# A Hymba-style encoder block: paired rests turned in the bank of the fourth turned tile, an earlier low-rank load, reordered steps, and more bridging products

## The chip, the cores and the metric

One Trainium2 chip; the kernel runs on one of its cores. The metric is the device time of one execution in microseconds. The kernel before takes 905.07 us, the median of 3 runs (904.97 to 905.77).

## What is computed

One layer over 512 tokens of width 2048, in float32. A condition vector gives shift, scale and gate; the normalised and modulated input is projected once, and the columns go to two mixers, dilated sliding-window attention (16 heads of 64) and gated linear attention (4 heads, GLA below). Both are gated, joined and projected out.

```python
mod = jax.nn.silu(c) @ w_cond[layer] + b_cond[layer]
shift, scale, gate = jnp.split(mod, 3, axis=-1)
h = rms_norm(x) * (1.0 + scale[:, None]) + shift[:, None]
proj = h @ w_in[layer]
aq, ak, av, ag, gq, gk, gv, gg, lr_f, lr_b = jnp.split(proj, PROJ_SPLITS, axis=-1)
...
for window, dilation in DILATED_PATTERNS:        # (128,1), (512,4), (2048,16)
    o_p, lse_p = dilated_window_attention(aq, ak, av, rel_bias, window, dilation)
...
g_o = rms_norm(o_fwd + o_bwd).reshape(B, S, GLA_WIDTH) * gla_norm_gain[layer]
g_out = g_o * jax.nn.silu(gg)
y = jnp.concatenate([a_out, g_out], axis=-1) @ w_out[layer]
x = x + gate[:, None] * y
return rms_norm(x) * final_gain
```

## The kernel before

**Units.** Every large product is a unit: PE accumulates four tiles of 128 x 512 in PSUM over the 16 slices of the depth. Operands are split into a high and a low part in fp32r, and one product is three matmuls (three(), L229 to L232: high by high, low by high, high by low). PSUM has two pools: PJ with five banks (four hold the sums of the running unit, one is for other tiles) and PA with three (L214 to L218).

**Stages.** By the time of PE: a start with the condition sums and the first projection products, "sta", to about 96 us and "stb" to about 187; the attention beside the units qk2, qk4, qk6 and gk, about 190 to 444; the V unit with the low-rank product, to about 538; the units ag0, ag1, gg0 and gg1 with the GLA heads beside them, to about 744; the output products, to 897, and a tail.

**Beside a unit** run side items. Each has a place between 0 and 1, the share of the unit's product triples ahead of it. PE's order is that of the program text (a manual schedule); DVE, ACT, POOL and SP are put in order by a scheduler from the dependences between tiles, except in the start, which is planned by hand.

**The attention** (attention(), L818) has per head h four score tiles s{h}{i} (score(), L829), each 128 queries by 416 keys: two matmuls, a biased sum and a row maximum on DVE (L847), the exponential on ACT (L851), the scaling on POOL (L864). The result p{h}{i} then goes through turn(h, i), L868: three 128 x 128 transposes on PE (L882) into the first 384 columns of a PA bank t{h}{i}, a copy of them to the high part pth on ACT (L888), and the remainder ptl = t − pth on DVE (L889). The 32 columns of each tile that are left over are kept paired in p{h}0. They are turned once per head by rest(h), L896, called from turn(h, 3): one transpose (L899) into a PJ bank of its own, r{h}; then, for each of two pairs of 32-row pieces, two copies on ACT (L906) and two subtractions on DVE (L908). The pairs are in series through pth and ptl, which they write. values(h), L910, multiplies with pth and ptl into o{h} (L915).

**The low-rank load.** Behind gk, lrb is loaded through SP (L1303), split on ACT (L1306) and DVE (L1307), and used beside the V unit.

**GLA.** gla_head(h), L1012, returns its ten items with their places: GLA_FIRST for head 0, GLA_AT for heads 1 to 3 (L121, L122). turn(d) transposes the keys (kt, L1062), states(d) multiplies keys with values (kv, L1074), outs(v) makes the output (go, L1123).

**The start.** warm(n), L293, issues n matmuls of 128 x 512 on constants, whose result nobody reads; warm(6) (L324) stands ahead of the first products of "sta" (L591), which need h_hi, the modulated input (L534).

Of the kernel before, what the change touches and what calls it, by code (L numbers as in the profile page):

```python
# [18 lines left out]
P = 128  # L19
S = 512  # L20
D = 2048
KT = D // P
# [95 lines left out]
REST_OF = (14, 11, 2, 15)  # L118
TOKENS = [slice(256 * c + a, 256 * c + 256, 2) for a in range(2) for c in range(2)]

GLA_AT = (0.01, 0.02, 0.33, 0.46, 0.46, 0.56, 0.64, 0.76, 0.76, 0.88)  # L121
GLA_FIRST = (0.3, 0.38, 0.55, 0.62, 0.775, 0.81, 0.86, 0.9, 0.92, 0.97)  # L122

SUMS_IN = {"ag0": 8, "ag1": 8, "gg0": 8}

# [66 lines left out]
def block_kernel(ctx: ExitStack, tc: tile.TileContext, a: dict):  # L192
    nc = tc.nc
# [14 lines left out]
    def T2(name, dt=F32, parts=P):  # L208
        return t2.tile([parts, 512], dt, tag="t2", name=name)
# [4 lines left out]
    def PJ(name):  # L214
        return pp.tile([P, 512], F32, tag="pj", bufs=5, name=name)

    def PA(name):
        return pp.tile([P, 512], F32, tag="pa", bufs=3, name=name)  # L218
# [74 lines left out]
    def warm(n):  # L293

        for _ in range(n):
            mm(psw, hot[:, :P], hot, start=True, stop=True)
# [4 lines left out]
    with tc.manual_schedule(engines=PLANNED):  # L301
        small_inputs()
        cond_load(0, 0)
        half_load(0)
        x_load(0)
        half_load(1)
        nc.scalar.preload_act_table_set("silu_and_others")
        nc.vector.memset(hot.bitcast(F32), 1.0)
        nc.vector.memset(epst, EPS)
        nc.vector.memset(ch.bitcast(F32), 0.0)  # L310
        nc.vector.memset(sel.bitcast(F32), 0.0)
        nc.gpsimd.memset(cl.bitcast(F32), 0.0)
        warm(5)

        nc.vector.tensor_copy(ch[:4], cin[:, :512])
        act(sel[:4], cin[:, 512:], AF.Copy)
        tt(cl[:4], cin[:, :512], ch[:4].bitcast(F32), op=ALU.subtract)

        nc.vector.tensor_scalar(bcond[:, 16:32], bcond[:, 16:32], 1.0, None, op0=ALU.add)
        for j in range(4):  # L320
            spread(j, ch, True)
            spread(j, cl, False)
            act(sb[:, 512 * j:512 * j + 512], pcs[j], AF.Silu)
        warm(6)  # L324

    def cond_sum(dst, w, with_, init):

# [327 lines left out]
    for z in range(2):  # L655
        c = slice(512 * z, 512 * z + 512)
# [43 lines left out]
    for i in range(n):  # L700
        if i > 15:
            mm_task(i)
        st, k, j = chain[i]
# [14 lines left out]
    for i in range(n, 2 * n):  # L718
        mm_task(i)
        st, k, j = chain[i]  # L720
# [21 lines left out]
    ident = const("ident", [P, P])  # L742
# [75 lines left out]
    def attention(pairs):  # L818

        tiles = [(2 * p + j, i) for p in pairs for j in range(2) for i in range(4)]  # L820
        gt, pr_, held_parts = {}, {}, []
# [46 lines left out]
        def turn(h, i):  # L868
            def go():
                if not pts:  # L870
                    for z in "hl":
                        pts.append(B8(f"pt{z}", [16, P], F32R))
                        for at, to in ((2, 3), (11, 12)) + ((14, 16),) * (z == "h"):
                            nc.gpsimd.memset(pts[-1][:, at:to, :].bitcast(F32), 0.0)
                if i == 3:
                    rest(h)
                t = pr_.pop((h, i)) if i else pr_[h, i]
                pk = PA(f"t{h}{i}")
                first_ = 0 if i % 2 else 128
                for n_, (c, _) in enumerate(FULL[i]):  # L880
                    kt = (c - i - 1) % 4
                    nc.tensor.transpose(pk[:, n_ * P:n_ * P + P], t[:, first_ + kt * P:first_ + kt * P + P], ident)  # L882
                at, step = FULL[i][0][1], FULL[i][1][1] - FULL[i][0][1]
                hi, lo = (pt[:, at:at + 2 * step + 1:step, :] for pt in pts)
                src = pk[:, :3 * P].rearrange("p (k q) -> p k q", k=3)

                def parts():
                    act(hi, src, AF.Copy)  # L888
                    tt(lo, src, hi.bitcast(F32), op=ALU.subtract)  # L889
                if i or h == heads[0]:  # L890
                    parts()
                else:
                    held_parts.append(parts)
            return go

        def rest(h):  # L896

            pk = PJ(f"r{h}")
            nc.tensor.transpose(pk[:, :P], pr_.pop((h, 0))[:, 0:128], ident)  # L899
            hi, lo = pts  # L900
            to = [(hi, 0, hi, 32), (hi, 0, lo, 0), (hi, 96, lo, 96), (hi, 64, hi, 96)]
            parts = [(t[a:a + 32, REST_OF[i], :], u[b:b + 32, REST_OF[i], :], pk[96 - 32 * i:128 - 32 * i, :P])
                     for i, (t, a, u, b) in enumerate(to)]
            for pair in (parts[:2], parts[2:]):
                for up, _, of in pair:
                    act(up, of, AF.Copy)  # L906
                for up, low_, of in pair:
                    tt(low_, of, up.bitcast(F32), op=ALU.subtract)  # L908
# [103 lines left out]
    def gla_head(h):  # L1012
# [4 lines left out]
        def gates(d):  # L1017
            def go():
                n = f"{h}{d}"
                bias = gbias[:, 4 * d + h:4 * d + h + 1]  # L1020
                pz = PA("z" + n)
                mm(pz, gla["up"][:, d, h * P:h * P + P], gla["lr"], start=True, stop=True)
                e = T2("e" + n)
                act(e, pz, AF.Abs, bias=bias)
                act(e, e, AF.Exp, scale=-1.0)
                act(e, e, AF.Ln, bias=1.0)
                g = T2("g" + n)
                nc.vector.tensor_scalar(g, pz, bias, 0.0, op0=ALU.add, op1=ALU.min)  # L1028
                tt(g, g, e, op=ALU.subtract)
                b = T2("b" + n)  # L1030
                rst = gla["rst"]
                if d == 0:
                    nc.vector.tensor_tensor_scan(b, rst, g, 0.0, op0=ALU.mult, op1=ALU.add)
                    im, il = 63, 127
                else:
                    nc.vector.tensor_tensor_scan(b[:, ::-1], rst, g[:, ::-1], 0.0,
                                                 op0=ALU.mult, op1=ALU.add)
                    im, il = 64, 0
                b3 = b.rearrange("p (n t) -> p n t", n=4)
                sc = gs.tile([P, 3, 4], F32, tag="sc", name="sc" + n, bufs=4)  # L1040
                act(sc[:, 0, :], b3[:, :, im], AF.Exp, scale=1.0 / 16)
                act(sc[:, 1, :], b3[:, :, il], AF.Exp, scale=1.0 / 16)
                bm = T2("bm" + n)
                bm3 = bm.rearrange("p (n t) -> p n t", n=4)
                tt(bm3, b3, b3[:, :, im:im + 1].to_broadcast([P, 4, P]), op=ALU.subtract)
                act(sc[:, 2, :], bm3[:, :, il], AF.Exp, scale=1.0 / 16)
                qi = T2("qi" + n)
                ki = T2("ki" + n)
                act(ki, bm, AF.Exp, scale=-1.0 / 16)
                act(qi, bm, AF.Exp, scale=1.0 / 16)  # L1050
                gq, gk = gla["q"][:, h, :], gla["k"][:, h, :]
                tt(ki, ki, gk, op=ALU.mult)
                tt(qi, qi, gq, op=ALU.mult)
                dirs[d].update(qi=qi, ki=ki, sc=sc, order=[0, 1, 2] if d == 0 else [3, 2, 1])
            return go

        def turn(d):
            def go():
                n, x = f"{h}{d}", dirs[d]
                pk = PA("kt" + n)  # L1060
                for j, c in enumerate(x["order"]):
                    nc.tensor.transpose(pk[:, j * P:j * P + P], x["ki"][:, c * P:c * P + P], ident)  # L1062
                x["kit"] = T2("kit" + n)
                act(x["kit"][:, :384], pk[:, :384], AF.Copy)
            return go
# [65 lines left out]
        def norm():  # L1131
# [10 lines left out]
            for v in range(2):  # L1142
                m = 2 * h + v
                if m % 4 == 0:
# [2 lines left out]
                    op0=ALU.mult, op1=ALU.mult)  # L1147

        at = GLA_AT if h else GLA_FIRST
        return list(zip(at, [gates(0), gates(1), turn(0), turn(1), states(0), states(1), att,  # L1150
                             outs(0), outs(1), norm]))

    def urgent(go):
# [137 lines left out]
        for q in range(2):  # L1291
            qk_evict(p + 2 + q, ps[2 * q], ps[2 * q + 1])

    ps = unit("gk", False, attention((6, 7)))
    kp_.close()
    gs = mid.enter_context(tc.tile_pool(name="gs", bufs=1, reuse_waits="tile"))
    gla["k"] = B8("gkt", [4, 512])
# [1 line left out]
        act(gla["k"][:, i, :], ps[i], AF.Copy)  # L1299


    lrb = T2("lrb")
    nc.sync.dma_start(lrb.rearrange("p (k c) -> p k c", k=KT), a["w_lr"][0])  # L1303
    lrs = gp.tile([P, KT, 2, 32], F32R, tag="g", name="lrs")
    lrb3 = lrb.rearrange("p (k c) -> p k c", k=KT)
    act(lrs[:, :, 0, :], lrb3, AF.Copy)  # L1306
    tt(lrs[:, :, 1, :], lrb3, lrs[:, :, 0, :].bitcast(F32), op=ALU.subtract)  # L1307
    plr = PA("plr")
# [161 lines left out]
    def to_s1(z):  # L1470
        tt(part(z, 1), part(2 + z, 1), part(z, 1), op=ALU.subtract)

    def to_s2(z):
        stt(part(z, 0), part(z, 1), -1.0, part(z, 0), op0=ALU.mult, op1=ALU.subtract)
# [6 lines left out]
            (0.65, lambda: to_s1(0)), (0.8, lambda: to_s2(0))]  # L1481
    ps = unit("gg1", False, side + some_sums("gg1"))
    gate_evict(ps, cat[3], "g1")
    to_s1(1)
    to_s2(1)
    mid.close()
    op = ctx.enter_context(tc.tile_pool(name="op", bufs=1, reuse_waits="tile"))
    for e in "hl":
# [145 lines left out]
    def later(pair, prod, g, go):  # L1634
        todo.setdefault((pair, prod, g), []).append(go)
# [37 lines left out]
    for z in range(2):  # L1673
        later(0, "P4", 1 + 2 * z, lambda z=z: halves("A12", z, part(2 + z, 0))())
    later(0, "P1", 1, gate_row)
    later(0, "P4", 2, gain_rows(0))
    later(0, "P4", 3, x_again(0))
    later(1, "P7", 0, x_again(1))
# [129 lines left out]
```

## Time and profile before

| what | before |
|---|---|
| median of 3 runs | 905.07 us |
| the profiled execution, by its own time | 907.22 us |
| its span, first to last instruction | 905.4 us |
| mean granted clock of TensorE | 0.996 |
| PE busy | 890.0 us, 98% |
| DVE busy | 731.2 us, 81% |
| ACT busy | 491.6 us, 54% |
| POOL busy | 125.9 us, 14% |

In the profile PE is TensorE, PEld its weight load, DVE VectorE, ACT ScalarE, POOL GpSimd, SP the queue that issues most loads. A row of the timeline has the start in us, the length in us, engine, line, operation, out<-in by the program's names without their numbers (t stands for all t{h}{i}), shapes and count, and in brackets the idle time ahead of it and what ended it. A clock of 0.50 means that TensorE was granted half its pulses. The profiled execution is 1.8 us longer than its span and 2.15 above the median.

### The profile page before, as it was taken

Reading aid. Unit: us, or ns where it says so; the run is one execution under the profiler, and the core shown is the slowest. Engines: PE = TensorE matmul, PEld = TensorE weight load, DVE = VectorE, ACT = ScalarE, POOL = GpSimd, SP = SyncE. Lnnn points to the kernel's source line nnn. Section 1 sums busy time; section 2 is a strip of 40 time slices with the busy share of each in tenths; the row PEclk is TensorE's granted clock in tenths of the full one; section 3 lists DMA queues with packets and bytes.
Section 4 is the critical chain, followed back from the end, with each engine's and each line's share of the span. In section 5 each row is a group of like instructions: output and inputs, shape, how many; then the busy total and the mean of one; then the engine's idle time right before and its main releaser. Section 6 shows DMA issues by size and latency. Waiting matters only on the chain.

```text
span 905.4 us, 12339 instructions
## 1 busy us (share of the span) xinstructions
PE 890.0 (98%) x4159; PEld 739.2 (82%) x4159; DVE 731.2 (81%) x1220; ACT 491.6 (54%) x841; POOL 125.9 (14%) x219
## 2 busy tenths in 40 slices
PE   8999999999999999999999999999999999999996
PEld 6888788888888888887778888888888888888885
DVE  7998799878989989888568668595787559797687
ACT  5554533466655745655657554373664248455454
POOL 0000000023323333243000101112020100000001
PEclk9999999999999999999999999999999999999999
DMA  9999489398798898998778879778796988777863
GB/s 342 401 411 363 186 344 367 134 306 226 202 266 273 247 265 247 249 298 223 232 260 255 311 206 308 206 249 262 231 279 208 275 286 289 282 288 249 289 238 154
DMA packets 65547, 242.33 MB, mean 268 GB/s; under 512 B 9190, under 2 KB 11526, under 8 KB 55883
## 3 DMA queue, kind: packets, MB, share of 16 engines
q1 hardware_dynamic: 58724, 199.23, 61.5%
q0 software_dynamic: 6464, 42.01, 19.4%
q8 instruction: 33, 0.54, 0.2%
q10 hardware_dynamic: 296, 0.30, 0.1%
q14 instruction: 30, 0.25, 0.1%
HBM read 224.64 MB, written 51.47 MB: 305 GB/s over the span
## 4 chain that ended last, share of the span: by engine, by line
PE 91%; DVE 3%; ACT 2%; DMA 2%; issue 1%; SPq 0%; DVEq 0%; ACTq 0%
PE ps_qk L230 5%; PE ps_qk L232 5%; PE ps_qk L231 5%; PE g L232 4%; PE g L230 4%; PE g L231 4%; PE stb L232 3%; PE stb L231 3%; PE stb L230 3%; PE ps_ag L232 3%; PE ps_ag L230 3%; PE ps_ag L231 3%; PE o L915 3%; PE sta L230 3%; PE sta L231 3%; PE sta L232 3%
## 5 line engine op out<-in xcount | busy, mean ns | idle before, releaser
L864 POOL TENSOR_SCALAR p<-p,st 128x32 f32<-128x32 f32 (+2 forms) x108 | 59.8, 565 | 159.9 <-DVE st L854 91.2
L328 DVE CUSTOM_DVE_ANT_0 cb<-cb,sb,c_bcond 128x2048 f32<-128x2048 f32 (+1 forms) x32 | 73.4, 2295 | 1.9 <-DMA cb<-in_wm 1.6
L851 ACT ACTIVATE p<-p,st 128x416 f32<-128x416 f32 x64 | 41.0, 641 | 49.2 <-DVE st L847 42.3
L429 POOL DMA_DIRECT2D T<-in_w_o x32 | 23.2, 725 | 159.4 <-ACT V2h L493 14.8
L888 ACT ACTIVATE pth<-t 128x384 fp32r<-128x384 f32 x64 | 31.0, 485 | 19.8 <-PE t L882 11.1
L889 DVE TENSOR_TENSOR ptl<-t,pth 128x384 fp32r<-128x384 f32 x64 | 35.2, 551 | 5.2 <-ACT pth L888 3.7
L882 PE MATMUL t<-c_ident,p 128*128 128x128 f32 x192 | 31.3, 272 | 0.0
L882 PEld LDWEIGHTS t<-c_ident,p 128*128 128x128 f32 x192 | 24.3, 139 | 7.9
L847 DVE CUSTOM_DVE_ANT_0 p<-s,g,st 128x256 f32<-128x256 f32 x64 | 27.7, 432 | 1.8
L847 DVE CUSTOM_DVE_ANT_0 p<-s,g 128x160 f32<-128x160 f32 x64 | 23.5, 367 | 4.2 <-PE s L840 3.5
L328 DVE CUSTOM_DVE_ANT_0 rawg<-rawg,crow,gate 128x1024 f32<-128x1024 f32 x16 | 20.4, 1279 | 4.0 <-DMA rawg<-in_wg 4.0
L1581 POOL TENSOR_SCALAR x<-x,rn 128x512 f32<-128x512 f32 x2 | 2.3, 1167 | 148.5 <-ACT rn L1570 148.5
L429 POOL DMA_DIRECT2D T3V<-in_w_gv x8 | 5.5, 687 | 125.1 <-ACT qk21h L493 118.7
L839 PE MATMUL s<-ks,qh 128*128 128x416 f32 x64 | 22.6, 353 | 0.0
L906 ACT ACTIVATE pth<-r 32x128 fp32r<-32x128 f32 x64 | 17.2, 269 | 9.9 <-PE r L899 4.5
L840 PE MATMUL s<-ks,ql 128*128 128x416 f32 x64 | 22.4, 350 | 0.0
L1091 ACT ACTIVATE sq<-st,sc 128x256 f32<-128x256 f32 x24 | 12.2, 506 | 18.6 <-DVE st L1081 10.0
L328 DVE CUSTOM_DVE_ANT_0 rawg<-rawg,crow,c_bcond 128x1024 f32<-128x1024 f32 x16 | 20.3, 1279 | 0.5 <-DVE g L1028 0.5
L429 POOL DMA_DIRECT2D T<-T x16 | 9.1, 571 | 79.9 <-ACT V8h L493 12.9
L915 PE MATMUL o<-pth,vv 128*128 128x512 f32 (+1 forms) x64 | 15.9, 369 | 2.2 <-DVE pth L908 1.1
L466 DVE TENSOR_TENSOR raw_O<-raw_O,raw_P 128x1024 f32<-128x1024 f32 x8 | 9.8, 1225 | 10.1 <-DMA raw_O<-in_w_o 7.8
L568 ACT ACTIVATE h_hi<-xt,shift 128x512 fp32r<-128x512 f32 x16 | 11.5, 721 | 10.3 <-DVE shift L328 9.5
(1661 smaller groups left out, 3151.6 us busy)
## 6 DMA issues: line engine op xcount, KB each, us to landing
cb<-in_wm SPq DMA_DIRECT2D x31, 1024.0 KB, 9.3
T<-in_w_o POOLq DMA_DIRECT2D x32, 512.0 KB, 6.5
rawg<-in_wg SPq DMA_DIRECT2D x32, 512.0 KB, 5.4
raw_O<-in_w_o SPq DMA_DIRECT2D x32, 512.0 KB, 4.6
raw_qk<-in_w_qk SPq DMA_DIRECT2D x24, 512.0 KB, 4.9
raw_O<-T SPq DMA_DIRECT2D x24, 512.0 KB, 5.0
rawb<-in_w_sb SPq DMA_DIRECT2D x16, 512.0 KB, 8.9
rawv<-in_wv SPq DMA_DIRECT2D x16, 512.0 KB, 5.6
```

The lines of the kernel that those rows point to most:

```text
L230: mm(ps, lh, rh, start=first, stop=False, skip_group_check=more)
L231: mm(ps, ll, rh, start=False, stop=False, skip_group_check=more)
L232: mm(ps, lh, rl, start=False, stop=last, skip_group_check=more)
L328: return nc.vector.tensor_tensor_reduce(out=w, in0=w, in1=with_, op0=ALU.mult, op1=ALU.add, scale=1.0, scalar=init, accum_out=dst)
L429: move = nc.gpsimd.dma_start(dst, src, max_dma_last_dim=8192, **how).ins
L847: top = nc.vector.tensor_tensor_reduce(out=t[:, lo:hi], in0=ps[:, lo:hi], in1=gt[h][:, at:at + 2 * (hi - lo) - 1:2], op0=ALU.add, op1=ALU.min,
L851: act(t, t, AF.Exp, bias=st[:, 0:1], scale=-1.0, accum_out=st[:, 1:2])
L864: last["pool"] = nc.gpsimd.tensor_scalar(to, of, st[:, 2:3], 1.0, op0=ALU.mult, op1=ALU.mult).ins
L882: nc.tensor.transpose(pk[:, n_ * P:n_ * P + P], t[:, first_ + kt * P:first_ + kt * P + P], ident)
L888: act(hi, src, AF.Copy)
L889: tt(lo, src, hi.bitcast(F32), op=ALU.subtract)
L915: mm(po[:, P * a0:P * a1], vv[h // 4][:, c, h % 4, :], pt[:, at:at + (a1 - a0 - 1) * step + 1:step, :], start=n_ == z == 0, stop=False, sk ...
```

## The change

1. rest(h) becomes rest(h, pk): turn(h, 3) allocates the PA bank t{h}3 first and hands its last 128 columns to the rest. The PJ bank r{h} goes.
2. The load of lrb moves from behind gk to a side item of gk at 0.7.
3. In GLA heads 1 to 3 states(0) comes ahead of turn(1), by place .46 and .47; in head 0 the order stays, and the places of outs become 0.91 and 0.93.
4. to_s1(1) and to_s2(1) (sums of operands for the output products) are called from an item of the first output product instead of behind gg1.
5. warm(6) becomes warm(13).

```diff
-GLA_AT = (0.01, 0.02, 0.33, 0.46, 0.46, 0.56, 0.64, 0.76, 0.76, 0.88)
-GLA_FIRST = (0.3, 0.38, 0.55, 0.62, 0.775, 0.81, 0.86, 0.9, 0.92, 0.97)
+GLA_AT = (0.01, 0.02, 0.33, 0.46, 0.47, 0.56, 0.64, 0.76, 0.76, 0.88)
+GLA_FIRST = (0.3, 0.38, 0.55, 0.775, 0.62, 0.81, 0.86, 0.91, 0.93, 0.97)
...
-        warm(6)
+        warm(13)
...
+                pk = PA(f"t{h}{i}")
                 if i == 3:
-                    rest(h)
+                    rest(h, pk[:, 3 * P:])
                 t = pr_.pop((h, i)) if i else pr_[h, i]
-                pk = PA(f"t{h}{i}")
...
-        def rest(h):
-
-            pk = PJ(f"r{h}")
-            nc.tensor.transpose(pk[:, :P], pr_.pop((h, 0))[:, 0:128], ident)
+        def rest(h, pk):
+
+            nc.tensor.transpose(pk, pr_.pop((h, 0))[:, 0:128], ident)
             hi, lo = pts
             to = [(hi, 0, hi, 32), (hi, 0, lo, 0), (hi, 96, lo, 96), (hi, 64, hi, 96)]
-            parts = [(t[a:a + 32, REST_OF[i], :], u[b:b + 32, REST_OF[i], :], pk[96 - 32 * i:128 - 32 * i, :P])
+            parts = [(t[a:a + 32, REST_OF[i], :], u[b:b + 32, REST_OF[i], :], pk[96 - 32 * i:128 - 32 * i, :])
                      for i, (t, a, u, b) in enumerate(to)]
...
-        return list(zip(at, [gates(0), gates(1), turn(0), turn(1), states(0), states(1), att,
+        return list(zip(at, [gates(0), gates(1), turn(0), states(0), turn(1), states(1), att,
...
+    lrb = []
+
+    def lr_load():
+        lrb.append(T2("lrb"))
+        nc.sync.dma_start(lrb[0].rearrange("p (k c) -> p k c", k=KT), a["w_lr"][0])
+
-    ps = unit("gk", False, attention((6, 7)))
+    ps = unit("gk", False, attention((6, 7)) + [(0.7, lr_load)])
...
-    to_s1(1)
-    to_s2(1)
...
+    later(0, "P1", 1, lambda: (to_s1(1), to_s2(1)))
```

The built programs show what moves. First PE, at head 12, beside the unit gk (ps_gk); p is the probabilities' tile, t the turned one, and the brackets name the engines that a row waits for. Before:

```order
L230 MATMUL ps_gk_3671<-h_hi,gk3h 128x512
L231 MATMUL ps_gk_3671<-h_hi,gk3l 128x512
L232 MATMUL ps_gk_3671<-h_lo,gk3h 128x512
L899 MATMUL r_3894<-c_ident,p_3734 128x128 [waits Pool_49]
L882 MATMUL t_3904<-c_ident,p_3817 128x128 [waits DVE_49,PE_49,Activation_49]
L882 MATMUL t_3904<-c_ident,p_3817 128x128 x2
L230 MATMUL ps_gk_3672<-h_hi,gk3h 128x512
```

After:

```order
L230 MATMUL ps_gk_3666<-h_hi,gk3h 128x512
L231 MATMUL ps_gk_3666<-h_hi,gk3l 128x512
L232 MATMUL ps_gk_3666<-h_lo,gk3h 128x512
L898 MATMUL t_3889<-c_ident,p_3729 128x128 [waits DVE_49,PE_49,Pool_49]
L882 MATMUL t_3889<-c_ident,p_3812 128x128 [waits DVE_49,Activation_49]
L882 MATMUL t_3889<-c_ident,p_3812 128x128 x2
L230 MATMUL ps_gk_3667<-h_hi,gk3h 128x512
```

The four transposes stand in the same places, but all write t now, and the wait for the bank's former reader has moved to the first of them (L898). The second (L882) still waits for DVE. Counted through DVE's instructions, it waited before for the former reader of its bank, and waits after for the last of the rest's four subtractions.

On ACT, the same head: pth<-r and pth<-t of 32x128 are the rest's copies. Before:

```order
L493 ACTIVATE gk5h<-raw_gk_3795 128x1024
L851 ACTIVATE p_3872,st_3873<-p_3872,st_3873 128x416
L906 ACTIVATE pth<-r_3894 32x128 x2
L888 ACTIVATE pth<-t_3904 128x3x128
L906 ACTIVATE pth<-r_3894 32x128 x2
L851 ACTIVATE p_3916,st_3917<-p_3916,st_3917 128x416
```

After:

```order
L493 ACTIVATE gk5h<-raw_gk_3790 128x1024
L851 ACTIVATE p_3867,st_3868<-p_3867,st_3868 128x416
L905 ACTIVATE pth<-t_3889 32x128 x4
L888 ACTIVATE pth<-t_3889 128x3x128
L851 ACTIVATE p_3910,st_3911<-p_3910,st_3911 128x416
```

The copy of t stood between the rest's pairs and now stands behind all four. The same on DVE, where before the scores' work (L847) came between the subtractions:

```order
L908 TENSOR_TENSOR pth<-r_3894,pth 32x128
L908 TENSOR_TENSOR ptl<-r_3894,pth 32x128
L889 TENSOR_TENSOR ptl<-t_3904,pth 128x3x128
L847 ISA p_3916,st_3917<-s_3913,g_3751 128x160
L847 ISA st_3917 128x1
L908 TENSOR_TENSOR ptl<-r_3894,pth 32x128
L847 ISA p_3916,st_3917<-s_3913,g_3751,st_3917 128x256
L847 ISA st_3917 128x1
L908 TENSOR_TENSOR pth<-r_3894,pth 32x128
```

After:

```order
L907 TENSOR_TENSOR pth<-t_3889,pth 32x128
L907 TENSOR_TENSOR ptl<-t_3889,pth 32x128 x2
L907 TENSOR_TENSOR pth<-t_3889,pth 32x128
L889 TENSOR_TENSOR ptl<-t_3889,pth 128x3x128
L847 ISA p_3910,st_3911<-s_3907,g_3746 128x160
```

All four subtractions now come together, ahead of t's own and of the next scores.

More of the change, by code (lines that the diff above doesn't have):

```diff
@@ L1299, in block_kernel @@
         act(gla["k"][:, i, :], ps[i], AF.Copy)
-    lrb = T2("lrb")
-    nc.sync.dma_start(lrb.rearrange("p (k c) -> p k c", k=KT), a["w_lr"][0])
     lrs = gp.tile([P, KT, 2, 32], F32R, tag="g", name="lrs")
-    lrb3 = lrb.rearrange("p (k c) -> p k c", k=KT)
+    lrb3 = lrb[0].rearrange("p (k c) -> p k c", k=KT)
     act(lrs[:, :, 0, :], lrb3, AF.Copy)
```

## The prediction

> **What bounds the kernel now.** I read the page first, for the busy shares and for the chain that ended last.
>
> ```profile
> PE 890.0 (98%) x4159; PEld 739.2 (82%) x4159; DVE 731.2 (81%) x1220; ACT 491.6 (54%) x841; POOL 125.9 (14%) x219
> PE 91%; DVE 3%; ACT 2%; DMA 2%; issue 1%; SPq 0%; DVEq 0%; ACTq 0%
> ```
>
> TensorE is busy for 98% of the span and carries 91% of the chain. So any time in which PE stands still is added to the end, and a change can win only what PE idles now. The waits of PE's queue say how little that is:
>
> ```profile
> PE sta L591 <- ACT h_hi L534: 2.7, 1, 2.7
> PE o L915 <- DVE pth L908: 1.1, 1, 1.1
> PE o L915 <- ACT pth L888: 1.0, 1, 1.0
> PE go L1123 <- ACT V27h L493: 0.3, 1, 0.3
> ```
>
> One wait at the start, two at the value products o of the attention, one in the linear attention: 5.1 us in all. Next I read the windows of two stretches of the attention, where 16 heads run beside the unit products.
>
> ```profile
> 352.00:382.00 30.00, 29.99 (x149) 25.09 (x148) 27.89 (x66) 19.20 (x42) 8.34 (x15) 1.00 0.87 234
> 412.00:442.00 30.00, 28.20 (x142) 23.23 (x140) 22.24 (x64) 18.52 (x45) 7.03 (x13) 1.00 0.80 230
> ```
>
> The columns are the length, then busy us of PE, its weight load, DVE, ACT and POOL, and the granted clock. In the first stretch PE is never idle and DVE works 27.89 of 30 us: any short chain through DVE and ACT queues there, and today nobody waits for it. What the change does to that chain decides the result.
>
> **The rest's bank, the heaviest part.** Per head, rest() transposes the paired rests once, copies four 32-row pieces on ACT and subtracts each on DVE. The timeline of head 12 shows the whole chain:
>
> ```profile
> 398.35 0.27 PE L899 MATMUL r<-c_ident,p 128*128 128x128 f32 x1
> 398.46 0.49 PE L882 MATMUL t<-c_ident,p 128*128 128x128 f32 x3
> 398.71 0.48 PE L230 MATMUL ps_gk<-h_hi,gk3h 128*128 128x512 f32 x1
> 399.00 0.55 ACT L906 ACTIVATE pth<-r 32x128 fp32r<-32x128 f32 x2
> 399.58 0.49 ACT L888 ACTIVATE pth<-t 128x384 fp32r<-128x384 f32 x1
> 399.59 0.29 DVE L908 TENSOR_TENSOR pth<-r,pth 32x128 fp32r<-32x128 f32 x1
> 399.90 0.28 DVE L908 TENSOR_TENSOR ptl<-r,pth 32x128 fp32r<-32x128 f32 x1
> 400.22 0.56 ACT L906 ACTIVATE pth<-r 32x128 fp32r<-32x128 f32 x2
> 401.04 0.29 DVE L908 TENSOR_TENSOR ptl<-r,pth 32x128 fp32r<-32x128 f32 x1
> 401.89 0.28 DVE L908 TENSOR_TENSOR pth<-r,pth 32x128 fp32r<-32x128 f32 x1
> ```
>
> PE starts r at 398.35 and the first turned tile t 0.11 us later; the unit product follows at 398.71. PE waits for nothing. ACT's second pair starts only after DVE's second subtraction (400.18, then 400.22), so the four steps are in series, and the last ends 3.82 us after r started (401.89 + 0.28 − 398.35).
>
> The change puts the rest into the spare quarter of the fourth turned tile's bank. Its transpose comes first, the three transposes of t next, into the same tile. In the built order the first of these now waits for DVE; counting DVE's instructions up to the value it waits for gives the fourth subtraction, in each of the 16 heads. The rows on the change show the consequence: ACT's four copies and DVE's four subtractions now stand ahead of t's own copy and subtraction, which is only needed if t comes after them all. Columns do not overlap, but the tile is one. PE runs in order, so behind the waiting transpose are queued the other two, the unit's products and the next scores; all stop for the length of the chain.
>
> Its length, lower end: nothing queued. r 0.27 and 0.03 to the start of ACT, copies 0.56, then 0.04, subtractions 0.29 + 0.29, 0.04, copies 0.56, 0.04, subtractions 0.58: 2.7 us, less the 0.11 that lies between r and t today: 2.6 of stall. Upper end: what is queued in front. For head 12, ACT was busy until 398.98, and with today's rows in the new order the fourth subtraction would end near 401.4, a stall of 2.9. Head 0 is worse:
>
> ```profile
> 208.65 0.56 ACT L906 ACTIVATE pth<-r 32x128 fp32r<-32x128 f32 x2 [0.58 <-PE r L899]
> 209.54 0.69 DVE L1228 TENSOR_TENSOR S1e<-h_lo 128x512 f32<-128x512 f32 x1
> 210.26 0.29 DVE L908 TENSOR_TENSOR pth<-r,pth 32x128 fp32r<-32x128 f32 x1
> 213.36 0.28 DVE L908 TENSOR_TENSOR pth<-r,pth 32x128 fp32r<-32x128 f32 x1
> ```
>
> There DVE takes the first subtraction at 210.26, 1.05 us after the copies, behind a sum over tokens. In the new order 0.58 + 0.04 + 0.56 + 0.04 + 0.58 follow: 212.1, or 3.75 us after r (which starts 0.3 ahead of ACT, at 208.35), a stall of 3.6. A stopped PE feeds DVE nothing new, which pulls toward the lower end; DVE at 27.89 of 30 pulls up. I take 3.2 a head, between the two heads: 16 × 3.2 = **51 us**, bounds 16 × 2.6 = 42 and 16 × 3.6 = 58. It covers no work: all unit products stand behind it.
>
> What it relieves is small. The o waits above (2.1) are for these same subtractions and copies; they would be done by then.
>
> **The clock after a stall.** Windows of 3.41 us at the start and at the end show what idle time does:
>
> ```profile
> 7.87:11.28 3.41, 1.03 (x5) 0.84 (x6) 2.81 (x6) 2.23 (x5) 0.00 (x0) 1.00 1.03 407
> 11.28:14.69 3.41, 3.41 (x10) 2.64 (x9) 2.31 (x3) 1.00 (x2) 0.00 (x0) 0.50 1.03 429
> 14.69:18.10 3.41, 3.41 (x16) 2.82 (x15) 3.04 (x6) 2.00 (x4) 0.00 (x0) 1.00 1.01 408
> 895.33:898.74 3.41, 1.59 (x7) 0.97 (x6) 2.31 (x6) 2.23 (x6) 0.99 (x1) 1.00 0.26 102
> 898.74:902.15 3.41, 0.00 (x0) 0.00 (x0) 2.10 (x5) 2.01 (x6) 0.00 (x0) 1.00 0.78 310
> ```
>
> After a window with 2.38 us of idle (3.41 − 1.03) the clock was 0.50 for one window, with 10 products in place of 16; after one with 1.82 idle it stayed 1.00. So the limit T lies between. A stall of 3.2 us at a random phase puts T or more into one window with a chance of (3.41 + 3.2 − 2T) / 3.41: 54% at 2.38, 87% at 1.82. I take 70%, 11 stalls. A half-clock window loses at most 1.7 us, by the counts 6/16 of 3.41 or 1.3; 1.5 taken: **16 us**, bounds 0 and 16 × 1.7 = 27.
>
> The Trainium skill, "TensorE: Matmul & The Clock Gate", section "What's actually happening", says that the clock halves after at least one idle window of some 3.4 us in a free-running count. Taken strictly, a 3.2-us stall never fills one, and this term would be zero. The row at 7.87 speaks against the strict reading: that window held 1.03 us of work, and the next ran at 0.50.
>
> **Thirteen bridging products, not six.** They run before the first product that needs the statistics.
>
> ```profile
> 6.08 1.52 PE L296 MATMUL warm<-hot 128*128 128x512 f32 x6
> 10.25 1.21 PE L591 MATMUL sta<-sa0hi,h_hi 128*128 128x512 f32 x4 [2.65 <-ACT h_hi L534]
> 15.55 0.94 ACT L534 ACTIVATE h_hi<-xt,scale 128x256 fp32r<-128x256 f32 x2
> 17.44 1.07 PE L591 MATMUL sta<-sa1hi,h_hi 128*128 128x512 f32 x4
> ```
>
> Started 0.227 us apart, seven more take 1.6 of the 2.65 idle, so 1.07 remain and nothing is delayed. That is under the 1.82 which kept the clock, so the half-clock window goes: 6/16 × 3.41 = 1.3 to 1.7, say 1.5. Late next is the second h_hi: PE takes it today at 17.44, and would reach it near 15.9, while its two halves are ready at 16.0 and 16.5; 0.3 comes back. Gain **1.2**, bounds 0 and 1.7.
>
> **The low-rank load beside gk.** Today ACT stands 2.78 us on it, and the last head's o waits behind:
>
> ```profile
> 441.12 0.63 ACT L1306 ACTIVATE lrs<-lrb 128x512 fp32r<-128x512 f32 x1 [2.78 <-DMA lrb<-in_w_lr]
> 440.92 0.39 PE L232 MATMUL ps_gv_P<-V0l,h_hi 128*128 128x512 f32 x1
> 442.31 0.96 PE L915 MATMUL o<-pth,vv 128*128 128x512 f32 x3 [1.01 <-ACT pth L888]
> ```
>
> Issued inside the unit gk, several loads earlier on SP, it is there in time for the last head: its o gains 1.2 (442.31 − 440.92 − 0.23). ACT's split of it also moves up, ahead of V0's, so ACT can stand there instead, for at most the 6.6 us that the load takes now:
>
> ```profile
> DMA to landing us min/median/max: 6.6/6.6/6.6
> ```
>
> Most of that would lie inside stalls of PE. Cost 0, upper end the same 2.8 as today.
>
> **The other orders.** The product of keys and values comes one product triple before the second turn in heads 1 to 3, and head 0's outputs come one triple, 0.69 us, later: at best the 0.3 of the go row, at worst the same again. The to_s1 and to_s2 calls land at the same place in every engine's built order: 0.
>
> **Sum.** Gains 1.2 + 2.1 + 0.3 = 3.6. The span 905.4 − 3.6 + 51 + 16 = 968.8. The profiled execution, 907.22, is its span and 1.8 around it, and 2.15 above the median; so the median is forecast 905.07 + 63.4 = **968.5**.
>
> **The rivals.** *The wait, with the clock kept.* If only a window nearly without work throttles, 905.07 − 3.6 + 51 = 952.5. For it: the clock stays 1.00 through every window of the attention, and 3.2 is less than a window. Against: the row at 7.87. 30%. The Trainium skill's page named above gives this outcome by its rule.
>
> *The wait does not stand in the way: faster.* If the DVE count that t waits for is already reached when PE gets there, as that of an earlier reader of the bank is today, r costs no more than now, and only the gains remain: 905.07 − 3.6 = 901.5. It decides at a wait under 3.6 / 16 = 0.22 us a head, less than one 0.29-us subtraction. For it: the columns are disjoint. Against: the place of the copies on ACT and DVE, and a chain of 2.6 us at its shortest. 5%.
>
> *Stalls that queue longer*, at 3.8 and more, as head 12's chain has today (3.82), each throttled: 905.07 − 3.6 + 61 + 27 = 989. 5%.
>
> **How the numbers follow.** The forecast keeps 60%. Its own bounds: 42 + 0.54 × 16 × 1.3 − 3.6 = 50 gives 955; 58 + 0.87 × 16 × 1.7 − 3.6 = 78 gives 983. Taking in the second case at its low end, 905.07 − 3.6 + 42 = 943.5, the range is 944 to 984. Faster by over 0.2% (1.8 us, about what a measurement of this kernel can tell from no change): 0.05; within: 0.02; slower: 0.93.
>
> **What would show it.** Right: PE's waits list the fourth turned tile's transposes (t, L882) released by DVE's pth of L907, 16 times, 45 to 58 us in all; windows at 0.50 in the attention, about 11; the stages behind the attention unchanged in length; the first half-clock window gone. Wrong: no such row in PE's waits, or PE still at 29.99 of 30 in the attention; or such rows with the clock at 1.00 throughout, which would be the second case.

## The result and the profile after

The changed kernel takes 990.91 us (median of 4, 989.82 to 993.12), the kernel before 905.4 in the same series: a ratio of 1.0945 with a 95% interval of 1.0929 to 1.0962. It is slower, by 85.5 us where 63.4 were forecast, and lies 7 us above the range.

The page of the changed kernel, with engine shares and the chain that ended last:

```profile
span 991.3 us, 12361 instructions
PE 923.3 (93%) x4166; PEld 761.9 (77%) x4166; DVE 733.2 (74%) x1220; ACT 492.6 (50%) x841; POOL 121.4 (12%) x219
PE 80%; DVE 9%; ACT 5%; DMA 3%; issue 2%; POOL 0%; SPq 0%; DVEq 0%; ACTq 0%; POOLq 0%
```

DVE and ACT now hold 14% of the chain, where they had 5%. PE's busy time rose by 33.3 us for seven more products (1.6 us): it works slower, and not only less often. The waits of PE's queue name the rest:

```profile
PE t L882 <- DVE pth L907: 55.0, 16, 4.2
PE kv L1073 <- ACT kit L1063: 2.6, 1, 2.6
PE warm L296 <- DVE hot L308: 1.5, 1, 1.5
```

The first row is the forecast's, in all 16 heads: 55.0 us. The waits of o and of the start have gone. The second row was not forecast.

Two heads in the timeline (start us, length us, engine, line, operation; idle time in brackets). Head 1 has one of the shortest waits:

```profile
227.41 0.27 PE L898 MATMUL t<-c_ident,p 128*128 128x128 f32 x1
227.87 0.56 ACT L905 ACTIVATE pth<-t 32x128 fp32r<-32x128 f32 x2
228.47 0.29 DVE L907 TENSOR_TENSOR pth<-t,pth 32x128 fp32r<-32x128 f32 x1 [0.43 <-ACT pth L905]
228.78 0.28 DVE L907 TENSOR_TENSOR ptl<-t,pth 32x128 fp32r<-32x128 f32 x1
229.16 0.55 ACT L905 ACTIVATE pth<-t 32x128 fp32r<-32x128 f32 x2 [0.72 <-DVE ptl L907]
229.74 0.29 DVE L907 TENSOR_TENSOR ptl<-t,pth 32x128 fp32r<-32x128 f32 x1 [0.68 <-ACT pth L905]
230.04 0.28 DVE L907 TENSOR_TENSOR pth<-t,pth 32x128 fp32r<-32x128 f32 x1
230.48 0.65 PE L882 MATMUL t<-c_ident,p 128*128 128x128 f32 x3 [2.79 <-DVE pth L907]
```

The four steps stand in series with almost nothing between, and PE starts 0.16 us after the last subtraction. In head 4 other work of DVE comes first:

```profile
294.53 0.56 ACT L905 ACTIVATE pth<-t 32x128 fp32r<-32x128 f32 x2 [0.64 <-PE t L898]
295.06 0.38 DVE L847 CUSTOM_DVE_ANT_0 p<-s,g,st 128x160 f32<-128x160 f32 x1
295.37 1.22 DVE L997 CUSTOM_DVE_ANT_0 rawv<-rawv,shb 128x1024 f32<-128x1024 f32 x1
296.70 0.29 DVE L907 TENSOR_TENSOR pth<-t,pth 32x128 fp32r<-32x128 f32 x1
298.64 0.56 PE L882 MATMUL t<-c_ident,p 128*128 128x128 f32 x3 [4.15 <-DVE pth L907]
```

The copies ended at 295.09, but a score's maximum and a bias row (1.22 us) held DVE to 296.67, so this wait is 4.15.

Now the clock, in windows of 3.41 us around two waits (length, busy us of PE, PEld, DVE, ACT and POOL, the granted clock, and the DMA's share and GB/s). The windows are laid so that the clock changes at their edges; the last two rows are from a third wait:

```profile
312.61:316.03 3.42, 1.48 (x7) 0.91 (x6) 2.66 (x10) 1.70 (x6) 1.41 (x4) 1.00 0.66 213
316.03:319.44 3.41, 2.54 (x8) 2.27 (x9) 1.13 (x3) 0.95 (x3) 0.00 (x0) 0.50 0.46 153
319.44:322.85 3.41, 3.41 (x11) 2.71 (x11) 2.63 (x7) 1.44 (x3) 0.21 (x1) 0.50 0.00 0
322.85:326.27 3.42, 3.42 (x18) 2.97 (x17) 1.59 (x6) 1.11 (x3) 0.66 (x3) 1.00 0.49 155
432.08:435.49 3.41, 1.68 (x10) 1.10 (x8) 2.97 (x6) 3.12 (x7) 0.25 (x1) 1.00 1.09 335
435.49:438.91 3.42, 1.59 (x9) 1.40 (x10) 2.06 (x6) 1.30 (x4) 0.00 (x0) 1.00 0.91 189
438.91:442.32 3.41, 3.41 (x18) 2.92 (x17) 2.31 (x5) 2.61 (x5) 0.00 (x0) 1.00 1.08 204
503.76:507.17 3.41, 2.88 (x9) 2.43 (x10) 0.93 (x3) 0.49 (x1) 1.54 (x3) 0.50 1.01 273
507.17:510.59 3.42, 3.42 (x19) 2.92 (x18) 0.99 (x5) 1.33 (x4) 0.00 (x0) 1.00 0.67 115
```

A window with 1.48 us of work is followed by half clock; one with 1.59 or 1.68 is not. And a half-clock window with 2.54 us of work is followed by a second, one with 2.88 is not. In all, 21 windows of the attention ran at 0.50, from 15 of the 16 waits (the rows from 432.08 are the one that split evenly over two windows), and six of the 15 cost two windows.

Stage by stage, the unit qk2 starts at 185.7 (187.2 before), the V unit at 523.0 (439.8), ag0 at 619.8 (537.7), gg1 at 784.9 (700.3). So the attention is 84.7 us longer, gg0 2.6, and the rest agrees within 1.5.

### The profile page after: what moved, and what is told of

Same layout as the page of the kernel before. It is cut to its first block, busy times and chain, and to the rows that moved or that the text cites. A ratio compares the mean times of both kernels' runs of the same rounds, so it can differ in the third digit from the quotient of the medians.

```text
span 991.3 us, 12361 instructions
## 1 busy us (share of the span) xinstructions
PE 923.3 (93%) x4166; PEld 761.9 (77%) x4166; DVE 733.2 (74%) x1220; ACT 492.6 (50%) x841; POOL 121.4 (12%) x219
## 4 chain that ended last, share of the span: by engine, by line
PE 80%; DVE 9%; ACT 5%; DMA 3%; issue 2%; POOL 0%; SPq 0%; DVEq 0%; ACTq 0%; POOLq 0%
PE ps_qk L230 4%; PE ps_qk L231 4%; PE ps_qk L232 4%; PE g L232 3%; PE g L230 3%; PE g L231 3%; PE stb L232 3%; PE stb L231 3%; PE stb L230 3%; PE ps_ag L230 3%; PE ps_ag L232 3%; PE ps_ag L231 3%; PE ps_gv_P L231 3%; PE ps_gv_P L230 3%; PE ps_gv_P L232 3%; PE sta L231 3%
## 5 line engine op out<-in xcount | busy, mean ns | idle before, releaser
L882 PE MATMUL t<-c_ident,p 128*128 128x128 f32 x192 | 36.5, 305 | 55.0 <-DVE pth L907 55.0
L864 POOL TENSOR_SCALAR p<-p,st 128x32 f32<-128x32 f32 (+2 forms) x108 | 55.1, 518 | 239.8 <-DVE st L854 126.7
L882 PEld LDWEIGHTS t<-c_ident,p 128*128 128x128 f32 x192 | 26.6, 157 | 67.6 <-ACT pth L905 53.3
L889 DVE TENSOR_TENSOR ptl<-t,pth 128x384 fp32r<-128x384 f32 x64 | 35.4, 553 | 32.2 <-ACT pth L888 30.1
L888 ACT ACTIVATE pth<-t 128x384 fp32r<-128x384 f32 x64 | 30.9, 482 | 41.2 <-PE t L882 41.1
L847 DVE CUSTOM_DVE_ANT_0 p<-s,g 128x160 f32<-128x160 f32 x64 | 23.7, 370 | 35.5 <-PE s L840 34.0
L847 DVE CUSTOM_DVE_ANT_0 p<-s,g,st 128x256 f32<-128x256 f32 x64 | 27.7, 433 | 2.1
L905 ACT ACTIVATE pth<-t 32x128 fp32r<-32x128 f32 x64 | 17.1, 268 | 16.6 <-DVE ptl L907 10.8
L840 PE MATMUL s<-ks,ql 128*128 128x416 f32 x64 | 24.4, 382 | 0.0
L1358 DVE TENSOR_TENSOR vS<-rawS,vS 128x1024 fp32r<-128x1024 f32 x8 | 9.7, 1223 | 9.8 <-ACT vS L1357 9.7
```

The source lines that it names most:

```text
L847: top = nc.vector.tensor_tensor_reduce(out=t[:, lo:hi], in0=ps[:, lo:hi], in1=gt[h][:, at:at + 2 * (hi - lo) - 1:2], op0=ALU.add, op1=ALU.min,
L864: last["pool"] = nc.gpsimd.tensor_scalar(to, of, st[:, 2:3], 1.0, op0=ALU.mult, op1=ALU.mult).ins
```

## The experiments

**The rest in its own bank.** All else as in the changed kernel.

```diff
-                pk = PA(f"t{h}{i}")
                 if i == 3:
-                    rest(h, pk[:, 3 * P:])
+                    rest(h, PJ(f"r{h}")[:, :P])
                 t = pr_.pop((h, i)) if i else pr_[h, i]
+                pk = PA(f"t{h}{i}")
```

> The changed kernel with one thing undone: the rest is turned into a bank of its own again. Theory (the turned tile's transposes wait for the rest's fourth subtraction, and the stalls halve the clock): both the 55.0 us of that wait and the half-clock windows of the attention go; what is left is the start (-1.9), the last head's o (about -1.2) and the new wait of kv on ACT's kit (+2.6), so 904 to 906 us. Rival (a good part of the 85 us comes from the other edits, the reorderings and the moved load): 915 us or more.

Measured: 908.23 us against 905.31, ratio 1.0027 (1.0018 to 1.0036). Its waits:

```profile
PE kv L1073 <- ACT kit L1063: 2.6, 1, 2.6
PE warm L296 <- DVE hot L308: 1.5, 1, 1.5
PE o L914 <- DVE pth L907: 1.1, 1, 1.1
PE sta L591 <- ACT h_hi L534: 0.2, 1, 0.2
```

With the bank go the 16 waits, and 82.7 of the 85.5 us. The bank is the cause. But the kernel is 2 to 4 us slower than expected: the other edits do not win, they lose 2.9.

**The rest last in the shared bank.** The same columns, the order of the transposes reversed.

```diff
-                if i == 3:
-                    rest(h, pk[:, 3 * P:])
...
                     nc.tensor.transpose(pk[:, n_ * P:n_ * P + P], t[:, first_ + kt * P:first_ + kt * P + P], ident)
+                if i == 3:
+                    rest(h, pk[:, 3 * P:])
```

> The changed kernel with the rest in the same columns of the same bank, but its transpose issued behind the three of the turned tile. Theory (it is the order of writes to one tile, not the shared bank, that stops PE): no wait of t on DVE's pth, 904 to 906 us, within 1 us of the kernel with a bank of its own. Rival (the shared bank itself costs, since it is held until the fourth subtraction and scores and turned tiles wait for one of the three banks): 0.5 to 1 us a head more, 912 to 921 us.

Measured: 918.71 us, ratio 1.0146 (1.0129 to 1.0163). The 16 waits are gone although the columns are shared, so it was the order of the writes to one tile that stopped PE. But 10.5 us remain against the own bank, within the rival's range and outside the theory's. The waits name another mechanism than the rival's, though:

```profile
PE o L914 <- ACT pth L888: 4.2, 6, 1.6
PE kv L1073 <- ACT kit L1063: 2.6, 1, 2.6
PE o L914 <- DVE ptl L889: 1.6, 3, 0.7
PE s L839 <- DVE ptl L889: 1.4, 1, 1.4
```

L888 and L889 are the turned tile's own copy and remainder. They stood behind the rest's, and o waited for them nine times, 5.8 us in all; waits for a bank (s for L889) are 1.4. PE's busy time is also 4.8 us above that with the own bank (895.7 and 890.9), which these rows do not explain.

**The same, with the turned tile's copy listed first.** rest() is called behind the tile's own copy, and only its transpose stays in place.

```diff
-                    rest(h, pk[:, 3 * P:])
+                    nc.tensor.transpose(pk[:, 3 * P:], pr_.pop((h, 0))[:, 0:128], ident)
...
                     held_parts.append(parts)
+                if i == 3:
+                    rest(h, pk[:, 3 * P:])
```

> The rest last in the shared bank, and its copies and subtractions listed behind those of the turned tile. Theory (the 10 us of the shared bank with the rest last come from the turned tile's own copy, which ACT takes behind the rest's four copies so that o waits for it): those o waits go, 908 to 911 us. Rival (the bank is held too long whatever the order): 916 us or more.

Measured: 911.67 us, ratio 1.0067 (1.0052 to 1.0083), 0.7 above the theory's range. One row is left of the o waits:

```profile
PE kv L1074 <- ACT kit L1064: 2.6, 1, 2.6
PE o L915 <- ACT pth L906: 2.0, 2, 1.4
```

Of the 10.5 us, 7 came from the order on ACT and DVE. The o row, 2.0, is now a wait for the rest's copies instead. Some 3 us against the own bank remain, and this trace cannot explain them: its execution took 907.97 us, 3.7 under the median, while the other three took 911.17 to 912.61. Their cause stays open.

**Work in the wait.** Twelve idle products between the rest's transpose and the tile's three.

```diff
                     rest(h, pk[:, 3 * P:])
+                    fl = PJ(f"fl{h}")
+                    for _ in range(12):
+                        mm(fl, onesr, h_hi[:, 0, :], start=True, stop=True)
```

> The changed kernel with 12 idle products of 128x512 (12 x 0.227 = 2.7 us) issued between the rest's transpose and the three of the turned tile, so that PE works during the wait; no result uses them. Theory (the increase of PE's busy time by 33 us is the clock halved after stalls): the wait itself stays in length, the idle time falls from 55 to about 12 us, no window of the attention is at 0.50, and the time falls by the 21 half windows, 32 us: 957 to 962 us. Rival (PE is slower for another cause, such as the bank being read while it is written): 985 us or more, since the wait is as long as before.

Measured: 964.35 us, ratio 1.0642 (1.0625 to 1.0659), no half-clock window in the attention.

```profile
PE 939.9 (98%) x4358; PEld 775.6 (81%) x4358; DVE 733.0 (76%) x1220; ACT 493.3 (51%) x841; POOL 121.6 (13%) x219
PE t L885 <- DVE pth L910: 9.8, 11, 1.4
PE kv L1076 <- ACT kit L1066: 2.6, 1, 2.6
```

The wait is still there, now filled; the time falls by 26.6 us. So the clock as the cause of the slower products is shown, by an edit that only adds work. It missed the expected range by 2.4 us: less the 43.7 of the idle products, PE is busy for 896.2 us, 5.3 more than with the own bank. Some 1.5 of these are one half-clock window at 727.83, behind the wait of kv, which the traces of the changed kernel and of the own bank do not have; where the others arise was not separated.

**Half as much work in the wait.** Six products instead of twelve.

> The changed kernel with 6 idle products of 128x512 (1.36 us) issued in each of the 16 waits, no result uses them: the idle part of a wait falls from 2.8 to 4.2 us to 1.4 to 2.8. Theory (the clock halves after a window of 3.41 us with more than about 1.9 us idle): six waits stay under that limit, of the other ten some six pass it by their place in the window; 6 to 8 half-clock windows, 11 us over the kernel with 12 idle products: 971 to 979 us. Rival 1 (a whole window without work is needed): no half-clock window, 963 to 966 us. Rival 2 (any stop of over 1 us halves it): as the changed kernel, 986 us or more.

Measured: 971.65 us, ratio 1.0733 (1.0709 to 1.0757), within the theory's range, with 31.9 us of wait left and 5 half-clock windows in the attention, one under the expected 6 to 8. Windows of this kernel on both sides of the limit:

```profile
206.20:209.61 3.41, 1.61 (x8) 1.00 (x6) 2.70 (x8) 1.81 (x6) 0.85 (x2) 1.00 0.94 324
209.61:213.03 3.42, 2.80 (x14) 2.42 (x15) 2.15 (x8) 0.71 (x2) 0.00 (x0) 1.00 0.42 168
257.40:260.81 3.41, 1.32 (x8) 0.96 (x8) 2.16 (x6) 1.40 (x4) 0.00 (x0) 1.00 1.03 228
260.81:264.23 3.42, 3.42 (x10) 2.69 (x9) 1.99 (x4) 1.89 (x5) 0.00 (x0) 0.50 1.00 244
264.23:267.64 3.41, 3.41 (x18) 2.94 (x17) 2.55 (x3) 2.02 (x3) 0.00 (x0) 1.00 0.89 184
```

1.61 us of work kept the clock, 1.32 did not. Both rivals fall: a window need not be empty, and not every stop counts.

**Only the rest's bank, on the kernel before.** Parts 2 to 5 of the change left out.

> The kernel before with only the rest moved into the turned tile's bank. Theory: 905.4 + 55 of wait + 32 of clock - 2 to 4 of o waits that go = 987 to 991 us. Rival (the other edits add to the loss or take from it by more than 3 us): under 985 or over 994 us.

Measured: 985.68 us, ratio 1.0883 (1.0868 to 1.0898), 1.3 us under the theory's range; the wait of t is 54.2 us. So, by medians of two series, the other edits add 5.2 to the loss, more than the 3 us of the expectation's rival. 2.7 of these are the next experiment's; of the others one profile shows a part, 18 half-clock windows where the changed kernel has 21. They come from 12 of the 16 waits, and again six cost two windows. Why the windows fall so wasn't tried.

**Only the reordering of GLA, on the kernel before.**

```diff
-GLA_AT = (0.01, 0.02, 0.33, 0.46, 0.46, 0.56, 0.64, 0.76, 0.76, 0.88)
-GLA_FIRST = (0.3, 0.38, 0.55, 0.62, 0.775, 0.81, 0.86, 0.9, 0.92, 0.97)
+GLA_AT = (0.01, 0.02, 0.33, 0.46, 0.47, 0.56, 0.64, 0.76, 0.76, 0.88)
+GLA_FIRST = (0.3, 0.38, 0.55, 0.775, 0.62, 0.81, 0.86, 0.91, 0.93, 0.97)
...
-        return list(zip(at, [gates(0), gates(1), turn(0), turn(1), states(0), states(1), att,
+        return list(zip(at, [gates(0), gates(1), turn(0), states(0), turn(1), states(1), att,
```

> The kernel before with only the new places and order of the GLA items. Theory: kv waits 2.6 us on ACT's kit in one head, 2.6 to 4.3 us more than before, 908 to 909.5 us. Rival (that wait comes only with the moved load or the rest's bank): 905 us, no such row.

Measured: 908.33 us against 905.61, ratio 1.0031 (1.0020 to 1.0041), with the kv row of 2.6 in its waits. ACT's queue in the changed kernel shows why, in head 3:

```profile
752.77 0.51 ACT L1090 ACTIVATE sq<-st,sc 128x256 f32<-128x256 f32 x1 [0.73 <-DVE st L1080]
754.76 0.51 ACT L1090 ACTIVATE sq<-st,sc 128x256 f32<-128x256 f32 x1 [0.53 <-DVE st L1085]
756.76 0.51 ACT L1090 ACTIVATE sq<-st,sc 128x256 f32<-128x256 f32 x1 [1.49 <-DVE st L1085]
757.17 0.47 ACT L1063 ACTIVATE kit<-kt 128x384 f32<-128x384 f32 x1
757.70 1.13 PE L1073 MATMUL kv<-gv,kit 128*128 128x256 f32 x4 [2.58 <-ACT kit L1063]
```

The copy kit of the second turn now stands behind the scaled states sq of the first direction, the last of which waits 1.49 us for DVE. Before, both copies came ahead of them.

**Without the reordering.** The own bank, the thirteen products and the earlier load; the later calls of to_s1 and to_s2 stay, here and in the next run.

> Own bank for the rest again, and also the old places and order of the GLA items; what is left of the change is the thirteen bridging products and the earlier load. Theory (the reordered states put ACT's second kit copy behind the scaled states, so that kv of head 3 waits 2.6 us, in some executions with a half-clock window behind it): 3 to 5 us less than with the reorderings, 902 to 905 us, no kv row in PE's waits. Rival (the loss of the other edits lies in the start or the load): 907 us or more.

Measured: 905.8 us against 905.61, ratio 0.9999 (0.9990 to 1.0008). No kv row:

```profile
PE warm L296 <- DVE hot L308: 1.5, 1, 1.5
PE o L914 <- DVE pth L907: 1.1, 1, 1.1
PE sta L591 <- ACT h_hi L534: 0.7, 1, 0.7
PE go L1122 <- ACT V27h L493: 0.3, 1, 0.3
```

It is 2.4 us less than with the reordering, and level with the kernel before, 0.8 above the expected range.

**The load alone.** As the last, with warm(6).

> As the kernel without the reorderings, but with six bridging products: of the change only the earlier load is left. Theory (seven more products end the half-clock window of the start): 1.5 to 2 us more than with thirteen; against the kernel before 0.5 to 1.2 us less, 904 to 905 us. Rival (the start varies from execution to execution, and bridging is worth nothing in the median): the same as with thirteen, within 0.5 us.

Measured: 905.7 us, ratio 0.9998 (0.9989 to 1.0007): the rival. Neither the bridging products nor the load is worth a measurable time. The start of this run has 2.3 us of idle time and still no half clock; likewise in the run with the reordering alone, whose start and load are those of the kernel before:

```profile
8.50:11.91 3.41, 1.86 (x8) 1.52 (x9) 2.64 (x5) 2.57 (x5) 0.00 (x0) 1.00 1.00 409
11.91:15.33 3.42, 3.42 (x17) 2.84 (x16) 2.44 (x3) 1.37 (x3) 0.00 (x0) 1.00 1.02 428
438.00 0.63 ACT L1306 ACTIVATE lrs<-lrb 128x512 fp32r<-128x512 f32 x1 [1.11 <-DMA lrb<-in_w_lr]
439.70 0.96 PE L915 MATMUL o<-pth,vv 128*128 128x512 f32 x4
```

The windows are counted back in steps of 3.413 us from the change to half clock at the end of the run with the reordering alone (899.38). They begin at 8.50, where in the kernel before they begin at 7.87. So the wait is split over two windows, the emptier holds 1.86 us of work (1.74 in the run with the load alone, from 8.37), and the clock stayed 1.00. The load had ACT stand 1.11 us instead of 2.78, and the last head's o waited for nothing.

Why the bridging products win nothing can be read here too. They fill idle time and do not move its end: with the load alone, sta begins at 10.04 us, and with thirteen products (the run before it) at 10.23, in both when h_hi is there. What they could win is the half-clock window alone, and of the four traced executions with six products and this start (the kernel before, the rest's bank alone, the reordering alone, the load alone) only the first has one.

## Why the prediction was wrong, point by point

*The wait: right.* "In the built order the first of these now waits for DVE", up to "the fourth subtraction, in each of the 16 heads", is the row of 55.0 us, within the bounds of 42 to 58. Taken were 51, at 3.2 a head; measured are 2.8 to 4.2, mean 3.4. The guess that a stopped PE empties DVE's queue held in head 1, not in head 4. 4 us of the miss.

*The clock: right in kind, the term mis-sized.* The prediction took "70%, 11 stalls" and one window each at 1.5: 16 us. The limit was bounded by 1.82 and 2.38 us of idle time, and the middle of the chances was taken. It lies between 1.82 (3.41 − 1.59) and 1.93 (3.41 − 1.48), at the low end, where the prediction's own formula gives over 80%: 15 of 16 came, and 12 in the run with only the rest's bank. What it left out is the second window: a wait that reaches into the half-clock window leaves that one short of work too, and with 1.30 to 2.66 us of work the clock did not come back, while 2.88 and more brought it back. Six waits did this in the changed kernel, and six in the run with only the rest's bank. 21 windows × 1.5 = 32 us in the trace, beyond the term's upper bound of 27; 26.6 by the experiment with filled waits, which has some cost of its own. This is the step that failed, the count of half-clock windows: 11 taken, 21 in the trace, 11 to 16 of the 22 us.

*The rule of the clock page.* The Trainium skill, "TensorE: Matmul & The Clock Gate", section "What's actually happening", has the clock halve after at least one idle window. Taken strictly this would have given 952.5; the runs contradict it, since only two of the windows that throttled in the changed kernel held no work at all and the others up to 1.48 us. The free-running window of about 3.4 us agrees with the traces: the changes of the clock lie on a grid of 3.413 us, and it begins elsewhere in each run (7.87, 8.37 and 8.50 above).

*The other edits: wrong in sign.* Forecast was a gain of 3.6, measured a loss of 2.9 with the own bank. Two steps failed. "at best the 0.3 of the go row, at worst the same again" looked at PE's order only; the reordering also moved ACT's copy behind the scaled states, and costs 2.7. The 0.3 of the go row did come with it. And the gains of 1.2 at the start and 1.0 at the last head's o (part of the 2.1) came from stalls of one execution, whose own time was 2.15 us above the median. In the traced run of the reordering alone, with the same start and load, the half-clock window and the wait of the last o are not there, and the edits against them won nothing in the median (905.8 and 905.7 us against 905.61). The prediction had that difference in its sum and did not ask what it was made of. The other 1.1 of the 2.1 hung on the shared bank, as the prediction said: the row is gone in the changed kernel and back with the own bank.

*The rivals.* The one at 989, with waits of 3.8 and every one throttled, came nearest to the measured time, by luck: the waits were 3.4, and it too had one window for each. Its "each throttled" was nearly right.

*The load in ACT's way:* cost 0, as taken. *The to_s1 and to_s2 calls:* moved nothing, and weren't tried by themselves.

The three misses add up, by medians: 908.23 with the other edits (+2.9), 56.1 more to the filled waits, 26.6 more to the changed kernel. No version here beats the kernel before.

## What to carry to other kernels

A tile is one unit for its waits: before a second, disjoint part is put into it, ask which write comes second, and which readers of the first part it then waits for. On an in-order engine that is near full, a wait of 3 us costs 3 us and, where it takes enough out of a clock window, half of that again.

Before a stall seen in one profiled execution is counted as a gain, check whether that execution is slower than the median by about as much, and whether the stall hangs on a transfer or on a window's phase.

When two items change places, follow their copies on the other engines too: the new wait was on ACT, and PE's order did not show it.

## What the runs showed of the hardware

In the changed kernel the granted clock went to 0.50 after a window of 3.41 us with 1.48 us of TensorE work or less, and stayed 1.00 with 1.59 or more (1.32 and 1.61 on the two sides in the run with six idle products; 1.54 kept it in the run with only the rest's bank). At half clock it stayed there after a window with 2.66 us of work or less, and came back after 2.88 or more. So the limit for coming back is higher than that for losing it, and one stall of 3 to 4 us can cost two windows, 3 us.
